# A state-space mixer on one core: block transfers within SBUF, a Toeplitz product for the taps, states as the stationary side

## The chip, the cores and the metric

The kernel runs on one core of one Trainium2 chip. The metric is the device time of one execution in microseconds (us). TensorE (PE, weight loads PEld), VectorE (DVE), ScalarE (ACT), GpSimd (POOL) and SyncE (SP) have their own instruction queues; each queue runs in order and waits on semaphores.

## The reference, cut to what matters

The network has two blocks over 256 tokens of width 1024. Block 1 is attention, pooling and a mixture of 16384 experts. Block 2 is a chain: FFN 0, the S5 mixer, FFN 1, FFN 2, attention (MoBA), FFN 3. The change is in the S5 mixer, with its preparation in block 1:

```
u = h @ w_in                                  # 256 x 1024: 64 groups g of 16 channels n
state[t] = lambda * state[t-1] + B u[t]       # complex, 64 states per group, lambda = exp(a dt)
y[t] = Re(C state[t]) + d * u[t]
g = gelu(y);  g = g * sigmoid(g @ w_glu);  out = g @ w_out
```

Both kernels cut the 256 steps into 32 chunks c of 8 steps s. Within a chunk, y depends on u through 8 taps K[k] = Re(C lambda^k B), a 16x16 matrix per group and k. Between chunks only the state at a chunk's start counts: "contribution" makes each chunk's input to the state, "the recurrence" carries the state over the 32 chunks with lambda^8, and "states out" turns the states into their share of y.

## The kernel before, in words

All weights are streamed from HBM in units of 128x1024 float32 by SP (`Stream`, L61) into four buffers, and split in a high part `wh` (ACT, L74) and a low part `wl` (DVE, L75), so that a product is three matmuls (L317 to L319, `mode_a`). The stream runs ahead as far as the buffers allow.

`s5_prep` (L943) is a generator that runs beside the expert phase of block 1. It makes lambda and its powers `lam`, `cw` (C lambda^k), `me` (B for the contribution), the taps `kr` (L1093 to L1099) and the powers of lambda^8, `pr` and `pi`, on POOL. Its tiles live in the large tile `act_lo`, so a profile's row names `act_lo` for all of them.

`s5_mixer` (L1115) runs after FFN 0:
- `u_tile(f)`, eight times: 24 matmuls for 128 channels (8 groups), a DVE product with the norm (L1155) into `uT`, a transfer to a DRAM tile `u_dram` (L1157), and after four of them eight transfers back (L1162) as `us`, with the 8 steps by 16 channels of a group on the partitions. All on SP's queue.
- `tap_weights(f)`: block-diagonal 128x128 tap matrices `s5kb`, by ACT (L1141) or POOL (L1143). `taps(f)`: 8 matmuls of falling width (L1174), copied by ACT to `yc` (L1176).
- `contribution(hf)`: 64 matmuls per half of the groups (L1187), `us` moving; two ACT copies into `ee[hf]` (L1189).
- `chunks(hf)`: the recurrence of a half on DVE (L1198 to L1220), in two blocks of 16 chunks side by side: 16 steps of four small operations, then four operations on 480 columns that carry the first block's end into the second.
- `spread(hf)`: states into a zeroed tile `s5sbd` (ACT L1236, DVE L1234). `states_out(qt)`: 16 matmuls with `cw` stationary (L1245), an ACT copy (L1250), and eight transfers to `y_dram` (L1253, SP and POOL); `states_in` reads them back with channels on the partitions (L1257).
- Sum with `yc` (DVE L1310), gelu (ACT L1311), split (L249, L250), then the eight GLU tiles `s5gps`, their sigmoid (L1319), the product (L1321), and `w_out`.

From `u_tile(6)` to the last `states_in`, PE and DVE keep the order in which the code is written (`manual_schedule`); `run(a, b)` puts a operations of the first half's recurrence and b of the second's there, in turn. Elsewhere, and on the other engines, a scheduler places instructions by priority.

Of the kernel before, what the change touches and what calls it, by code (L numbers as in the profile page):

```python
# [11 lines left out]
F32 = mybir.dt.float32  # L12
# [9 lines left out]
P = 128  # L22
# [105 lines left out]
class Net:  # L128
# [4 lines left out]
    def __init__(self, ctx, tc, i, out, tap=None):  # L133
# [18 lines left out]
        self.v_order = [*range(self.NLO, P), *range(self.NLO)]  # L152
        self.ada_late = list(range(5, 5 + 8 * 5, 5))
# [158 lines left out]
    def mode_a(self, ps, w, xh, xl):  # L312

        wh, wl = w
        for k in range(KT):
# [627 lines left out]
    def s5_prep(self, lo, hi):  # L943
# [140 lines left out]
        yield kr_end  # L1084

# [16 lines left out]

        pr, pi = keep(15, Q), keep(15, 2, Q)
# [9 lines left out]
        self.s5 = (lam, cw, me, kr, grp, pr, pi)  # L1113

    def s5_mixer(self):  # L1115
        nc, tc, i = self.nc, self.tc, self.i
        Q = 32
        lam, cw, me, kr, grp, pr, pi = self.s5
        with ExitStack() as st:
            wp = st.enter_context(tc.tile_pool(name="s5w", bufs=1))  # L1120
            dp = st.enter_context(tc.tile_pool(name="s5d", bufs=1, space=bass.MemoryType.DRAM))
            u_dram = dp.tile([64, 16, 8, Q], F32, name="u_dram")
            y_dram = dp.tile([64, 16, 8, Q], F32, name="y_dram")
            xh, xl = self.gained(self.cols[:, self.MIX_G : self.MIX_G + KT])
            rx = self.rstd()
            row = None
            l8 = wp.tile([P, 2, 2, Q], F32, name="s5l8")
# [4 lines left out]
            kbs = {}  # L1132

            uT = wp.tile([P, KT, 8, Q], F32, tag="sA", name="s5uT")
            us = wp.tile([P, 64, Q], F32, tag="sB", name="s5us")
            def tap_weights(f):
                kb = wp.tile([P, 8, 8, 16], F32, tag="s5kb", name="s5kb", bufs=5)
                k = kr[:, f].rearrange("p (k n) -> p k n", n=16)
                if f % 2:
                    for g in range(8):  # L1140
                        nc.scalar.activation(kb[:, :, g], k, AF.Copy, scale=grp[:, g : g + 1])  # L1141
                else:
                    nc.gpsimd.tensor_mul(kb, k.unsqueeze(2).to_broadcast([P, 8, 8, 16]),  # L1143
                                         grp[:, 0:8].unsqueeze(1).unsqueeze(3).to_broadcast([P, 8, 8, 16]))
                kbs[f] = kb

            for f in (0, 2):
                tap_weights(f)
            def u_tile(f):
# [3 lines left out]
                if row is None:  # L1153
                    row = self.rstd_row(wp, rx)
                nc.vector.tensor_mul(uT[:, f], ps.rearrange("p (c s) -> p s c", s=8),  # L1155
                                     row.rearrange("p (c s) -> p s c", s=8))
                nc.sync.dma_start(u_dram[8 * f : 8 * f + 8].rearrange("g n s c -> (g n) (s c)"),  # L1157
                                  uT[:, f].rearrange("p s c -> p (s c)"))
                if f % 4 == 3:
                    gs = slice(8 * f - 24, 8 * f + 8)  # L1160
                    for s in range(8):
                        nc.sync.dma_start(us[16 * s : 16 * s + 16, gs], u_dram[gs, :, s].rearrange("g n c -> n g c"))  # L1162

            yc = wp.tile([P, KT, S], F32, name="s5yc")
# [3 lines left out]

            def taps(f):

                kb = kbs.pop(f)
                ps = self.pm.tile([P, S], F32, tag="m", name="s5yps")
                for k in range(8):
                    nc.tensor.matmul(ps[:, k * Q :], kb[:, k].rearrange("p a b -> p (a b)"),  # L1174
                                     uT[:, f, 0 : 8 - k].rearrange("p s c -> p (s c)"), start=(k == 0), stop=(k == 7))
                nc.scalar.activation(yc[:, f], ps, AF.Copy)  # L1176

            def contribution(hf):

                for b in range(2):  # L1180
                    ps = self.pa.tile([P, 2, 8, Q], F32, tag=f"acc{2 * hf + b}", name="s5eps")
                    for q8 in range(8):
                        q = 16 * hf + 8 * b + q8
                        for half in range(2):
                            hs = slice(64 * half, 64 * half + 64)
                            for r in range(2):
                                nc.tensor.matmul(ps[hs, r, q8], me[q // 8][:, q % 8, r, hs], us[:, 2 * q + half], start=True, stop=True,  # L1187
                                                 tile_position=(0, 64 * half))
                    nc.scalar.activation(ee[hf][:, :, :, 8 * b : 8 * b + 8].rearrange("p c r q -> p r q c"), ps, AF.Copy)  # L1189

            def chunks(hf):
# [3 lines left out]
                s4 = ss[hf].rearrange("p (b c) r q -> p b c r q", b=2)  # L1195
                e4 = ee[hf].rearrange("p (b c) r q -> p b c r q", b=2)
                bl = lambda a: a.unsqueeze(1).to_broadcast([P, 2, 2, 16])
                yield v.memset(s4[:, :, 0], 0.0)  # L1198
                for c in range(16):
                    n = 2 if c < 15 else 1  # L1200
                    t = wp.tile([P, 2, 2, 2, 16], F32, tag=f"s5t{hf}", name="s5t")
                    t0, t1 = t[:, 0, :n], t[:, 1, :n]
                    if c < 15:
                        yield v.tensor_mul(t0, bl(l8[:, 0, :, qs]), s4[:, :, c])
                        yield v.tensor_mul(t1, bl(l8[:, 1, :, qs]), s4[:, :, c, ::-1])
                        yield v.tensor_add(t0, t0, e4[:, :, c])
                        yield v.tensor_add(s4[:, :, c + 1], t0, t1)
                    else:
                        t0, t1, end = t0[:, 0], t1[:, 0], s4[:, 1, 0]
# [61 lines left out]
            for f in range(6):  # L1271
                u_tile(f)
                if f in (1, 3):
                    tap_weights(f)
# [326 lines left out]
```

## Time and profile before

| | |
|---|---|
| time, median of 3 runs | 2143.38 us (2139.41 to 2146.39) |
| the profiled execution | 2139.12 us |
| its span in the profile | 2137.3 us |
| mean granted TensorE clock | 0.984 |
| S5 mixer, first instruction to the GLU's third tile | about 1279 to 1384 us of the span |

Times in the rows further down are from the span's start. A timeline row gives start, duration, engine, line, operation, output<-inputs, shape, count, and in brackets how long the engine had been idle and what ended that. Rows that follow each other closely are merged: the duration is then that of the whole stretch.

### The profile page before, as it was taken

How to read it: one execution, taken by the hardware profiler on the slowest of the kernel's cores; microseconds unless marked ns; L12 is line 12 of the kernel's file. 1: busy time of each engine (PE TensorE's matmuls, PEld its weight loads, DVE VectorE, ACT ScalarE, POOL GpSimd, SP SyncE). 2: the span in 40 equal slices, each digit the busy share in tenths (PEclk: the TensorE clock that was granted, in tenths of full speed). 3: DMA queues.
4: the chain of work that ended last, by engine and by line, in shares of the span. 5: the costliest groups of instructions: out<-in, count | busy, mean ns of one | idle time of the engine just before them, and what ended most of it. 6: DMA issues, size and time to landing. Idle time of an engine off the chain costs nothing. (4 is left out here: it accounts for less than half of the span.)

```text
span 2137.3 us, 35377 instructions
## 1 busy us (share of the span) xinstructions
PE 2021.1 (95%) x13270; PEld 1816.1 (85%) x13270; DVE 1520.3 (71%) x2808; ACT 1024.1 (48%) x1609; POOL 540.2 (25%) x548
## 2 busy tenths in 40 slices
PE   6889899999999899999999998899999999999999
PEld 4667899999999677788889988789998999778998
DVE  7987489887989666998765557465556555776555
ACT  4663545443444444555554444454444444565443
POOL 2333003037999332000131121101111111210111
PEclk9999999999999999999999999899999999999999
DMA  8763355554444877555555535355555555444552
GB/s 333 251 228 109 121 186 177 178 170 154 151 158 149 271 254 233 178 188 186 178 177 187 181 126 129 99 166 179 181 190 162 180 187 187 148 138 148 187 180 97
DMA packets 129564, 378.69 MB, mean 177 GB/s; under 512 B 26897, under 2 KB 41281, under 8 KB 129266
## 3 DMA queue, kind: packets, MB, share of 16 engines
q1 hardware_dynamic: 128160, 372.71, 53.0%
q0 software_dynamic: 1232, 3.73, 0.6%
q8 instruction: 104, 1.70, 0.3%
q14 instruction: 66, 0.54, 0.1%
q10 hardware_dynamic: 2, 0.00, 0.0%
HBM read 366.95 MB, written 9.44 MB: 176 GB/s over the span
## 5 line engine op out<-in xcount | busy, mean ns | idle before, releaser
L75 DVE TENSOR_TENSOR wl<-raw,wh 128x1024 fp32r<-128x1024 f32 (+1 forms) x595 | 751.4, 1264 | 312.3 <-ACT wh L74 309.3
L74 ACT ACTIVATE wh<-raw 128x1024 fp32r<-128x1024 f32 (+1 forms) x628 | 661.3, 1055 | 469.6 <-PE gups L318 165.7
L317 PE MATMUL gups<-xh,wh 128*128 128x256 f32 x1408 | 398.5, 284 | 6.4 <-ACT xh L305 3.1
L318 PE MATMUL gups<-xl,wh 128*128 128x256 f32 x1408 | 399.6, 284 | 2.3 <-DVE xl L306 2.3
L319 PE MATMUL gups<-xh,wl 128*128 128x256 f32 x1408 | 399.3, 284 | 0.7 <-DVE wl L75 0.5
L893 POOL TENSOR_TENSOR sgl<-sgl,rrow 128x256 f32<-128x256 f32 x88 | 126.3, 1435 | 735.2 <-ACT sgl L892 735.2
L317 PE MATMUL ups<-xh,wh 128*128 128x256 f32 x1024 | 293.6, 287 | 0.3 <-ACT act_lo L752 0.2
L319 PE MATMUL ups<-xh,wl 128*128 128x256 f32 x1024 | 290.0, 283 | 0.0
L318 PE MATMUL ups<-xl,wh 128*128 128x256 f32 x1024 | 289.7, 283 | 0.0
L317 PEld LDWEIGHTS gups<-xh,wh 128*128 128x128 f32 x1408 | 268.1, 191 | 12.0 <-ACT xh L305 4.8
L318 PEld LDWEIGHTS gups<-xl,wh 128*128 128x128 f32 x1408 | 268.1, 190 | 6.7 <-DVE xl L306 3.1
L319 PEld LDWEIGHTS gups<-xh,wl 128*128 128x128 f32 x1408 | 268.3, 191 | 1.1 <-DVE wl L75 1.1
L326 PE MATMUL acc<-wh,gl 128*128 128x512 f32 x512 | 201.6, 396 | 7.5 <-DVE gl L250 7.5
L324 PE MATMUL acc<-wh,gh 128*128 128x512 f32 x512 | 202.0, 395 | 2.5 <-ACT gh L249 2.0
L676 POOL TENSOR_SCALAR ob<-iota,idxT 128x128 f32<-128x128 f32 x256 | 194.6, 778 | 36.4 <-PE ups L319 32.2
L317 PEld LDWEIGHTS ups<-xh,wh 128*128 128x128 f32 x1024 | 194.1, 190 | 0.8 <-ACT act_lo L752 0.7
L318 PEld LDWEIGHTS ups<-xl,wh 128*128 128x128 f32 x1024 | 193.9, 189 | 0.1
L319 PEld LDWEIGHTS ups<-xh,wl 128*128 128x128 f32 x1024 | 193.9, 189 | 0.1
L325 PE MATMUL acc<-wl,gh 128*128 128x512 f32 x380 | 149.6, 394 | 0.7 <-DVE wl L75 0.7
L324 PE MATMUL acc<-wh,hh 128*128 128x512 f32 x352 | 139.3, 396 | 3.7 <-ACT hh L249 3.7
L326 PE MATMUL acc<-wh,hl 128*128 128x512 f32 x352 | 138.2, 394 | 0.4 <-DVE hl L250 0.3
L325 PE MATMUL acc<-wl,hh 128*128 128x512 f32 x352 | 138.5, 393 | 0.0
(395 smaller groups left out, 3390.1 us busy)
## 6 DMA issues: line engine op xcount, KB each, us to landing
raw<-peer_u SPq DMA_DIRECT2D x128, 512.0 KB, 3.5
raw<-peer_v SPq DMA_DIRECT2D x128, 512.0 KB, 3.6
raw<-ffn_gate SPq DMA_DIRECT2D x88, 512.0 KB, 4.3
raw<-ffn_up SPq DMA_DIRECT2D x88, 512.0 KB, 4.3
raw<-ffn_down SPq DMA_DIRECT2D x88, 512.0 KB, 3.5
raw<-w_ada SPq DMA_DIRECT2D x48, 512.0 KB, 5.2
raw<-w_in SPq DMA_DIRECT2D x24, 512.0 KB, 4.5
raw<-moba_w_qkv SPq DMA_DIRECT2D x24, 512.0 KB, 3.5
```

Source lines behind the costliest of these rows:

```text
L74: nc.scalar.activation(h[:, :n], raw[:, :n], AF.Copy)
L75: nc.vector.tensor_sub(lo[:, :n], raw[:, :n], h[:, :n].bitcast(F32))
L317: self.nc.tensor.matmul(ps, wh[:, s], xh[:, k], start=(k == 0), stop=False)
L318: self.nc.tensor.matmul(ps, wh[:, s], xl[:, k], start=False, stop=False)
L319: self.nc.tensor.matmul(ps, wl[:, s], xh[:, k], start=False, stop=(k == KT - 1))
L324: mm(acc, lh, wh, start=start, stop=False)
L325: mm(acc, lh, wl, start=False, stop=False)
L326: mm(acc, ll, wh, start=False, stop=stop)
L676: nc.gpsimd.tensor_scalar(b, iota, idx[:, 1, n : n + 1], None, ALU.is_equal)
L893: nc.gpsimd.tensor_mul(sg, sg, row)
```

## The change

In `s5_prep`, a DRAM tile `toep_dram` of 8 x 128 x 8 x 128 is filled: seven blocks with zeros, then for each step s the taps, shifted right by 16 s columns. So row (s, channel) of group g holds what one step's input gives to all 8 later steps: a 128x128 Toeplitz matrix per group and f. `load_taps(hf)` loads half of it (2 MB) as `s5tt` by eight POOL transfers; there is one buffer for both halves.

`w_in`'s columns are reordered on the host, so that u leaves the matmul with (channel, group) on the partitions, and `gather` moves it by transfers within SBUF, from `uT` to `us`, in three batches (f 0 to 3, 4 to 6, 7). The last batch is issued half by ACT. `u_dram`, `y_dram`, `tap_weights`, `yc` and `spread` are gone. `taps(hf)` is 32 matmuls with `us` stationary (32 columns, the chunks) and the Toeplitz matrix moving (128 columns). `states_out(hf)` is 64 matmuls with the states stationary (64 rows, 32 columns) and `cw` moving, added in the same PSUM tiles. ACT applies gelu from PSUM, DVE turns 32x32 blocks (STREAM_TRANSPOSE) to bring channels back to the partitions, and the split follows, half by half. The recurrence runs in four blocks of 8 chunks, and three block ends are carried on.

```
+        gp.memset(tw, 0.0)
+        for s in range(1, 8):
+            nc.gpsimd.dma_start(self.toep[s].rearrange("p f k -> p (f k)"), tw.rearrange("p a b c -> p (a b c)"))
...
+        for s in range(8):
+            nc.gpsimd.dma_start(self.toep[s, :, :, 16 * s :], kr[:, :, : P - 16 * s])
...
+            def load_taps(hf):
+                toeplitz[hf] = wp.tile([P, 8, 4, P], F32, tag="s5tt", name="s5tt")
+                for s in range(8):
+                    nc.gpsimd.dma_start(toeplitz[hf][16 * s : 16 * s + 16],
+                                        self.toep[s, :, 4 * hf : 4 * hf + 4].rearrange("(g n) f k -> n g f k", n=16))
...
+                    nc.gpsimd.tensor_copy(pw[:, hf, 0, :, r], pr[:, :8, qs])
+                    nc.gpsimd.tensor_copy(pw[:, hf, 1, :, r], pi[:, :8, r, qs])
...
-                nc.sync.dma_start(u_dram[8 * f : 8 * f + 8].rearrange("g n s c -> (g n) (s c)"),
-                                  uT[:, f].rearrange("p s c -> p (s c)"))
...
+            def gather(f0, f1):
+                for s in range(8):
+                    q = nc.scalar if f1 == KT and s % 2 else nc.sync
+                    q.dma_start(us[16 * s : 16 * s + 16, :, f0:f1].rearrange("p g f c -> p g (f c)"),
+                                uT[:, s, f0:f1].rearrange("p f c -> p (f c)"))
...
+                for c in range(8):
+                    n = 4 if c < 7 else 3
...
+                    yield v.tensor_mul(t0, bl(l8[:, 0, :, qs]), s4[:, :n, c])
+                    yield v.tensor_mul(t1, bl(l8[:, 1, :, qs]), s4[:, :n, c, ::-1])
+                    yield v.tensor_add(t0, t0, e4[:, :n, c])
+                    yield v.tensor_add(s4[:, :, c + 1] if c < 7 else s4[:, 1:, 0], t0, t1)
...
+                for b in (1, 2, 3):
+                    yield v.tensor_copy(sw[:, b - 1], s4[:, b, 0, ::-1])
+                    if b < 3:
+                        yield v.tensor_mul(t[:, 0], pw[:, hf, 0, 7], s4[:, b, 0])
+                        yield v.tensor_mul(t[:, 1], pw[:, hf, 1, 7], sw[:, b - 1])
+                        yield v.tensor_add(t[:, 0], t[:, 0], t[:, 1])
+                        yield v.tensor_add(s4[:, b + 1, 0], s4[:, b + 1, 0], t[:, 0])
...
+                yield v.tensor_mul(x[:, 0], powers(pw[:, hf, 0]), flat[:, 1:, 0].unsqueeze(2).to_broadcast(sh))
+                yield v.tensor_mul(x[:, 1], powers(pw[:, hf, 1]),
+                                   sw.rearrange("p b r q -> p b (r q)").unsqueeze(2).to_broadcast(sh))
+                yield v.tensor_add(x[:, 0], x[:, 0], x[:, 1])
+                yield v.tensor_add(flat[:, 1:, 1:], flat[:, 1:, 1:], x[:, 0])
...
+            def taps(hf):
...
+                for half in range(2):
+                    ps = yps[hf, half] = self.pa.tile([P, 4, P], F32, tag=f"acc{2 * hf + half}", name="s5yps")
+                    for f in range(4):
+                        for j in range(4):
+                            nc.tensor.matmul(ps[32 * j : 32 * j + 32, f], us[:, 2 * j + half, 4 * hf + f],
+                                             toeplitz[hf][:, 2 * j + half, f], start=(f == 0), stop=False,
+                                             tile_position=(0, 32 * j))
+            def states_out(hf):
...
+                            for j in range(4):
+                                q = 4 * (4 * hf + f) + j
+                                nc.tensor.matmul(yps[hf, half][32 * j : 32 * j + 32, f], ss[hf][hs, :, r, q % 16],
+                                                 cw[q // 8][hs, r, q % 8, 1:9].rearrange("p a b -> p (a b)"),
+                                                 start=False, stop=(f == 3 and r == 1), tile_position=(64 * half, 32 * j))
+                yg = wp.tile([P, Q, 2, 16], F32, tag=f"sE{hf}", name="s5yg")
+                for half in range(2):
+                    nc.scalar.activation(yg[:, :, half], yps[hf, half].rearrange("p f (s n) -> p (f s) n", n=16),
+                                         AF.Gelu_apprx_tanh)
+                for f in (0, 2):
+                    fs = slice(4 * hf + f, 4 * hf + f + 2)
+                    nc.vector.transpose(yt[:, fs].rearrange("p f t -> p (f t)"),
+                                        yg[:, 8 * f : 8 * f + 16].rearrange("p a b c -> p (a b c)"))
+                    self.split(gh[:, fs], gl[:, fs], yt[:, fs])
...
+            for f in range(4):
                 u_tile(f)
+            gather(0, 4)
+            u_tile(4)
+            u_tile(5)
+            contribution(0)
             u_tile(6)
+            gather(4, 7)
+            run(6)
             u_tile(7)
+            gather(7, 8)
             taps(0)
+            load_taps(1)
+            run(24)
+            contribution(1)
             taps(1)
+            run(99, 17)
+            states_out(0)
             run(0, 99)
             states_out(1)
+            first = [(self.pm.tile([P, S], F32, tag="m", name="s5gps"), self.stream.next()) for _ in range(2)]
+            for ks in (range(4), range(4, KT)):
+                for ps, w in first:
+                    self.mode_a(ps, w, gh, gl, ks)
```

On SP's queue, around the projection of u, the rows before were these (`raw` is the weight stream):

```order
L61 DMA raw<-s_w_glu 128x1024
L1162 DMA s5us<-u_dram 16x32x32 x8
L1157 DMA u_dram<-s5uT 128x256 x3
L61 DMA raw<-s_w_glu 128x1024
L1157 DMA u_dram<-s5uT 128x256
L61 DMA raw<-s_w_glu 128x1024 x2
L1162 DMA s5us<-u_dram 16x32x32 x8
L61 DMA raw<-s_w_glu 128x1024
L1253 DMA y_dram<-s5ys 16x16x32 x10
```

and with the change, in the same place:

```order
L61 DMA raw<-s_w_in 128x1024 x8
L61 DMA raw<-s_w_glu 128x1024
L1171 DMA s5us<-s5uT 16x8x128 x8
L61 DMA raw<-s_w_glu 128x1024 x3
L1171 DMA s5us<-s5uT 16x8x96 x8
L1171 DMA s5us<-s5uT 16x8x32 x4
L61 DMA raw<-s_w_glu 128x1024
```

The eight writes and sixteen reads by way of DRAM have become twenty SBUF transfers (four more stand on ACT's queue), of 128 pieces each instead of 512.

On DVE, at the end of the recurrence's second half (`s5s` the states, `s5x` the carry, `s5yt` y by channels), the rows before were these:

```order
L1217 TENSOR_TENSOR s5x<-act_lo,s5s 128x480
L1218 TENSOR_TENSOR s5x<-act_lo,s5s 128x480
L1219 TENSOR_TENSOR s5s<-s5s,s5x 128x480
L1220 TENSOR_TENSOR s5s<-s5s,s5x 128x480
L1234 COPY s5sbd<-s5s 64x32x32
L1310 TENSOR_TENSOR s5yt<-s5yt,s5yc 128x256 x2
L250 TENSOR_TENSOR xl<-s5yt,xh 128x256 x2
```

With the change, these stand where the first half ends:

```order
L1206 TENSOR_TENSOR s5s<-s5t 128x4x32
L1224 TENSOR_TENSOR s5s<-s5s,s5x 128x3x224
L1255 STREAM_TRANSPOSE s5yt<-s5yg 128x512
L252 TENSOR_TENSOR xl<-s5yt,xh 128x512
L1255 STREAM_TRANSPOSE s5yt<-s5yg 128x512
L252 TENSOR_TENSOR xl<-s5yt,xh 128x512
L1203 TENSOR_TENSOR s5t<-s5l_13770,s5s 128x128
L1204 TENSOR_TENSOR s5t<-s5l_13770,s5s 128x128
```

The first half's turns and low parts (L1255, L252) now stand ahead of the last 31 operations of the second half's recurrence, which begin with L1203.

On POOL, between block 1 and FFN 0 (`x_sb` the residual, `sgl` FFN 0's gate), nothing stood before; with the change the taps' writes do:

```order
L480 TENSOR_TENSOR x_sb<-x_sb,upd 128x512 x2
L1109 DMA toep_dram<-act_lo 128x1024
L1109 DMA toep_dram<-act_lo 1024x1x112
L1109 DMA toep_dram<-act_lo 1024x1x96
L1109 DMA toep_dram<-act_lo 1024x1x80
L1109 DMA toep_dram<-act_lo 1024x1x64
L1109 DMA toep_dram<-act_lo 1024x1x48
L1109 DMA toep_dram<-act_lo 1024x1x32
L1109 DMA toep_dram<-act_lo 1024x1x16
L895 TENSOR_TENSOR sgl<-sgl,rrow 128x256 x22
L1139 DMA s5tt<-toep_dram 16x8x512 x8
```

Seven of the eight write 1024 pieces each, and FFN 0's first gate stands behind them.

## Rows read from the trace of the kernel before

**Rows 1.** Page, part 1: busy us, share of the span, instructions.

```profile
PE 2021.1 (95%) x13270; PEld 1816.1 (85%) x13270; DVE 1520.3 (71%) x2808; ACT 1024.1 (48%) x1609; POOL 540.2 (25%) x548
```

**Rows 2.** Engines by stretch: span, length, busy (instructions) per engine, clock, DMA share.

```profile
1340.60:1352.30 11.70, 9.07 (x48) 8.90 (x47) 10.81 (x48) 4.65 (x4) 0.00 (x0) 0.66 0.01 1
1352.30:1372.30 20.00, 16.57 (x129) 16.10 (x127) 0.99 (x4) 7.11 (x12) 6.77 (x12) 0.93 0.35 66
```

**Rows 3.** Timeline of DVE in the S5 mixer.

```profile
1282.19 1.45 DVE L1129 COPY s5l<-act_lo 128x32 f32<-128x32 f32 x2
1283.56 1.90 DVE L1130 TENSOR_SCALAR s5l<-act_lo 128x32 f32<-128x32 f32 x1
1285.38 0.17 DVE L1131 COPY s5l<-act_lo 128x32 f32<-128x32 f32 x1
...
1301.56 0.67 DVE L1155 TENSOR_TENSOR s5uT<-s5ups,rrow 128x256 f32<-128x256 f32 x1 [0.65 <-PE s5ups L319]
...
1307.25 0.67 DVE L1155 TENSOR_TENSOR s5uT<-s5ups,rrow 128x256 f32<-128x256 f32 x1 [0.64 <-PE s5ups L319]
...
1313.95 1.22 DVE L75 TENSOR_TENSOR wl<-raw,wh 128x1024 fp32r<-128x1024 f32 x1
...
1319.09 0.23 DVE L1204 TENSOR_TENSOR s5t<-s5l,s5s 128x64 f32<-128x64 f32 x1
...
1319.88 0.23 DVE L1204 TENSOR_TENSOR s5t<-s5l,s5s 128x64 f32<-128x64 f32 x1
...
1339.98 0.65 DVE L1220 TENSOR_TENSOR s5s<-s5s,s5x 128x480 f32<-128x480 f32 x1
...
1365.18 0.76 DVE L1310 TENSOR_TENSOR s5yt<-s5yt,s5yc 128x256 f32<-128x256 f32 x2 [12.71 <-DMA s5yt<-y_dram]
```

**Rows 4.** Timeline of PE: the preparation's last matmuls, and the S5 mixer.

```profile
1078.58 3.77 PE L1093 MATMUL tps<-act_lo,gate_hi 128*32 128x128 f32 x128
...
1313.52 3.93 PE L1187 MATMUL s5eps<-s5us,act_lo 128*64 128x32 f32 x128 [0.61 <-DMA u_dram<-s5uT]
...
1326.10 6.03 PE L1187 MATMUL s5eps<-s5us,act_lo 128*64 128x32 f32 x128 [3.94 <-DMA s5us<-u_dram]
...
1361.87 7.36 PE L1245 MATMUL s5sps<-s5sbd,act_lo 128*128 128x64 f32 x64 [0.41 <-ACT s5sbd L1236]
...
1384.12 0.38 PE L317 MATMUL s5gps<-xh,wh 128*128 128x256 f32 x1 [1.90 <-ACT s5sg L1319]
```

**Rows 5.** Timeline of SP's queue.

```profile
1299.40 0.32 SPq L1157 DMA_DIRECT2D u_dram<-s5uT  x1
...
1305.04 4.36 SPq L1162 DMA_DIRECT2D s5us<-u_dram  x8
```

**Rows 6.** DMA issues: output<-input, queue, count, KB each, median us to landing.

```profile
s5us<-u_dram SPq DMA_DIRECT2D x16, 64.0 KB, 4.4
...
y_dram<-s5ys SPq DMA_DIRECT2D x20, 32.0 KB, 2.0
```

**Rows 7.** Timeline of ACT in the S5 mixer.

```profile
1317.48 1.05 ACT L1189 ACTIVATE s5e<-s5eps 128x512 f32<-128x512 f32 x1 [0.74 <-PE s5eps L1187]
...
1351.99 0.60 ACT L1250 ACTIVATE s5ys<-s5sps 128x512 f32<-128x512 f32 x1 [6.89 <-PE s5sps L1245]
...
1381.31 1.06 ACT L74 ACTIVATE wh<-raw 128x1024 fp32r<-128x1024 f32 x1 [0.98 <-PE s5gps L318]
1382.38 1.28 ACT L1319 ACT_TABLE_LOAD   x1
```

**Rows 8.** Timeline of POOL: FFN 0's first gate, and the S5 mixer.

```profile
1099.35 0.74 POOL L893 TENSOR_TENSOR sgl<-sgl,rrow 128x256 f32<-128x256 f32 x1 [17.84 <-ACT sgl L892]
...
1279.71 5.72 POOL L1143 TENSOR_TENSOR s5kb<-act_lo 128x1024 f32<-128x1024 f32 x3 [4.15 <-PE acc L326]
...
1352.89 1.76 POOL L1253 DMA_DIRECT2D y_dram<-s5ys  x3 [28.64 <-ACT s5ys L1250]
```

**Rows 9.** Timeline of DVE: the last operations on the taps `kr`.

```profile
1084.02 0.67 DVE L125 SCALAR_TENSOR_TENSOR act_lo<-act_lo,cols_sb 128x16 f32<-128x16 f32 x4
```

More of the change, by code (lines that the diff above doesn't have):

```diff
@@ L310, in gained, with mode_a @@
         return xh, xl
-    def mode_a(self, ps, w, xh, xl):
+    def mode_a(self, ps, w, xh, xl, ks=range(KT)):
         wh, wl = w
-        for k in range(KT):
+        for k in ks:
             s = slice(k * P, k * P + P)
@@ L1112, in s5_prep @@
         gp.tensor_scalar(pi[:, :, 0], pi[:, :, 1], -1.0, None, ALU.mult)
-        self.s5 = (lam, cw, me, kr, grp, pr, pi)
+        self.s5 = (lam, cw, me, pr, pi)
     def s5_mixer(self):
@@ L1131, in s5_mixer @@
             nc.vector.tensor_copy(l8[:, 1, 1], lam[:, 1, 8])
[L1132 to L1148, printed above, removed]
+            pw = wp.tile([P, 2, 2, 8, 2, 16], F32, name="s5pw")
+            for hf in range(2):
+                qs = slice(16 * hf, 16 * hf + 16)
+                for r in range(2):
+                    nc.gpsimd.tensor_copy(pw[:, hf, 0, :, r], pr[:, :8, qs])
+                    nc.gpsimd.tensor_copy(pw[:, hf, 1, :, r], pi[:, :8, r, qs])
+            uT = wp.tile([P, 8, KT, Q], F32, tag="sA", name="s5uT")
+            us = wp.tile([P, 8, KT, Q], F32, tag="sB", name="s5us")
             def u_tile(f):
@@ L1167, in s5_mixer @@
             ss = [both[:, hf] for hf in range(2)]
[L1169 to L1176, printed above, removed]
             def contribution(hf):
@@ L1308, in s5_mixer @@
-            gh, gl = self.xt_tiles()
-            for f in range(KT):
-                nc.vector.tensor_add(yt[:, f], yt[:, f], yc[:, f])
-                nc.scalar.activation(yt[:, f], yt[:, f], AF.Gelu_apprx_tanh)
-                self.split(gh[:, f], gl[:, f], yt[:, f])
+            states_out(1)
             oh = wp.tile([P, KT, S], F32R, tag="sA", name="s5oh")
             ol = wp.tile([P, KT, S], F32R, tag="sS", name="s5ol")
-            for f in range(KT):
-                ps = self.pm.tile([P, S], F32, tag="m", name="s5gps")
-                self.mode_a(ps, self.stream.next(), gh, gl)
+            first = [(self.pm.tile([P, S], F32, tag="m", name="s5gps"), self.stream.next()) for _ in range(2)]
@@ L1318, in s5_mixer @@
+            for ks in (range(4), range(4, KT)):
+                for ps, w in first:
+                    self.mode_a(ps, w, gh, gl, ks)
+            in_order.close()
+            for f in range(KT):
+                if f < 2:
+                    ps = first[f][0]
+                else:
+                    ps = self.pm.tile([P, S], F32, tag="m", name="s5gps")
+                    self.mode_a(ps, self.stream.next(), gh, gl)
                 sg = wp.tile([P, S], F32, tag="s5sg", name="s5sg", bufs=2)
```

118 lines of the change are left out of this document (24 added, 94 removed).

## The prediction

> **What bounds the kernel now.** I read the page's busy shares first, then the stretches of the S5 mixer, then the timeline of each engine there. PE is busy for 95% of the span [rows 1], so elsewhere the kernel is paced by matmuls and the weight stream, which the change leaves alone. The mixer's middle is the exception. From 1340.60 to 1352.30 DVE is busy for 10.81 of 11.70 us: PE works at a granted clock of 0.66 and waits for the second half of the recurrence. From 1352.30 to 1372.30 DVE does 0.99 us of work in 20 [rows 2], and its next operation waits 12.71 us for y to come back from DRAM [rows 3]. Ahead of that, PE's second contribution waited 3.94 us for u to come back [rows 4]. The stage is a chain: u by way of DRAM, contribution, recurrence, states out, y by way of DRAM, gelu, GLU. So I follow that chain through the changed order to one mark: the first matmul of the GLU's third tile, which starts at 1384.12 [rows 4]. From there on both kernels do the same. Times below are on the axis of the trace of before.
>
> **The start of the mixer.** POOL's tap weights go (5.72 us [rows 8]); beside them two DVE copies took 1.45 us and the next 1.90, where the third, alone, took 0.17 [rows 3]. POOL now issues the taps' load there and copies eight small pieces. I take 2.8 us off (1.45 + 1.90 less three times 0.17); if the new POOL work holds DVE as the old did, it is nothing. ACT's 32 tap weights go too; they lay beside other work.
>
> **u.** `u_tile(3)`'s product ends at 1301.56 + 0.67 [rows 3], now 1299.4. Eight transfers follow on SP. An issue of 128 pieces took 0.32 us, one of 512 pieces 4.36 / 8 = 0.55 [rows 5]; the new ones have 128, I take 0.36, 2.9 in all. Landing: 2.0 us as the 32 KB writes, at most 4.4 as the reads of before [rows 6]. So u is there at 1304.3. PE ends `u_tile(5)` at 1307.25 [rows 3] less 2.8 = 1304.4, so contribution 0 need not wait; it takes 3.93 us [rows 4] and ends at 1308.4. Two more u tiles at 2.85 us each (1307.25 - 1301.56 is two tiles [rows 3]) end at 1311.2 and 1314.1.
>
> On DVE: the product of tile 6 until 1311.9, six recurrence operations, a low part of 1.22, the product of tile 7 until 1315.0. A step of four operations on 64 columns took 1319.88 - 1319.09 = 0.79 us; from 0.23 us at 64 columns to 0.65 at 480 [rows 3] a column costs 1.0 ns, so a step on 128 takes 1.05, an operation on 512 about 0.68 and one on 672 about 0.85. 24 operations (6.3) and eight more (1.4) end at 1322.7. The last batch of u is issued from 1315.0 (four each on SP and ACT, 1.4 us) and lands at 1318.4. PE did `taps(0)` meanwhile: 32 matmuls in the shape of the preparation's, 64 of which (two instructions each) took 3.77 us, 59 ns a matmul [rows 4], so 1.9 us until 1316.0. Contribution 1 took 3.93 us warm and 6.03 after an idle PE [rows 4]; I take 5, then ACT's copy of 1.05 [rows 7] and 0.1 of handoff: 1324.6. DVE then has 28 operations, both halves in turn: 14 on 128 columns at 0.2, ten small ones at 0.13 (an estimate, two thirds of that), four large ones at 0.8: 7.3 us. The first half's recurrence ends at 1331.9, against 1340.63 before (1339.98 + 0.65 [rows 3]).
>
> `taps(1)` has to be done by then. Its load is issued on POOL once `taps(0)` has freed the buffer, 8 x 0.59 (1.76 / 3 [rows 8]) = 4.7 us, 1320.7, with 4 us to land, 1325, then 1.9 to 2.9 on PE: hidden with 4 us to spare.
>
> **The tail.** Here the order matters: the turns of half 0 stand on DVE ahead of the rest of half 1.
> - States out 0: 64 matmuls. The trace has none with 64 rows and 32 columns; the nearest, 32 columns in four column groups, gives 59 ns, 3.8 us warm; the last of before, full width, 7.36 / 64 = 115 ns per instruction, two a matmul [rows 4], which is 14.7 us. I take the first, the nearer shape, and half of the cold surcharge of the contributions: 5.0. 1336.9.
> - Table load 1.28, then two gelus on 512 columns, 0.60 to 1.05 [rows 7], I take 0.8, and handoffs 0.2: 1340.0.
> - Turn, split, turn, split: DVE 4 x 0.68, ACT 2 x 0.60 [rows 7], handoffs 0.4: 4.3 us. A 32x32 turn is not in the trace; a copy's rate halved or doubled puts 0.34 to 1.36 on each of the two. 1344.3.
> - The 31 operations left of half 1, alone: four steps 4.2, eleven small ones at 0.2, four large ones 3.3: 9.7. 1354.0.
> - States out 1, PE cold: 5.8. Gelus 1.8, turns 4.3: 1365.9.
> - The low part of the GLU's second weight stands behind the turns: 1.2 [rows 3]. Then 24 matmuls until the first tile is whole, 0.12 us warm (2.85 / 24), 0.16 with a part of them cold: 3.8. Then ACT's 1.06 and 1.28 [rows 7] and 0.5 for the sigmoid: 1373.7 for the third tile.
>
> That is 10.4 us earlier. From the recurrence's end to the mark it was 43.5 us and is 41.8, so the 20 us of the round trip by DRAM are nearly all given back to the second half's recurrence, which now stands behind half 0's turns, and to a PE that cools beside it. What is won is won ahead of that.
>
> **Outside the mixer** I cost nothing. The zeros (3.7 MB) are written in the expert phase, where POOL has idle time. The taps are ready at 1084.7 (1084.02 + 0.67 [rows 9]) and FFN 0's first gate needs POOL at 1099.35 [rows 8]: eight issues at 0.59 fill 4.7 of 14.6 us. If an issue grows with its pieces, fourfold, it is 7 x 2.35 + 0.59 = 17 us, and FFN 0 starts 2.5 us later, since its first down product waits for that gate. The 7 x 1024 small writes share the DMA engines with the weights, eight units ahead there.
>
> **Sum.** 2139.1 (the profiled execution) - 10.4 = 2128.7. That execution lies 4.3 below the median of the runs shown, so against the median 2143.4 - 10.4 = 2133.0, my forecast. Low end: states out warm both times (-3.2), turns and gelus at their lower prices (-2.2), contribution 1 warm (-1.1), small operations overlapped better (-2), three more for handoffs and a warm GLU: 2121. High end with the mechanism intact: nothing at the start (+2.8), u landing as the reads of before and issues of 0.55 (+7.1 over both batches), turns and gelus high (+4), FFN 0 (+2.5): 2149.
>
> The Trainium skill, "DMA: Bandwidth & Descriptors", section Specifications, wants pieces of at least 512 bytes for line rate. In this trace the reads with pieces of 128 bytes landed in 4.4 us and the writes to DRAM with such pieces in 2.0 [rows 6], so it does not decide alone. By that rule the batches of 384 and 128 bytes would take the longer time: 2.4 us on the forecast.
>
> **Rivals.**
> 1. *The taps come late, no change.* POOL issues its load beside a busy DVE. For: DVE operations stretched from 0.17 to 1.90 beside POOL [rows 3]; if each of the eight issues is held as long (+1.73), they end at 1316.0 + 18.6 = 1334.6, the load lands at 1338.6, `taps(1)` ends at 1341.5, and states out 0 behind it on PE starts 9.6 later: 2142.6. Against: the rows show DVE held, not POOL's issue, and the three issues at 1352.89 had an idle DVE. The Trainium skill, "SBUF — State Buffer", section on a bandwidth-pool intuition that's wrong, has it that descriptors from GpSimd wait for a VectorE operation that holds the shared port, with 620 ns grown to 3100; by that figure the forecast would be some 14 us later, an estimate. No row here shows a POOL issue beside the recurrence.
> 2. *Slower: the state matmuls do not overlap.* Row groups of 64 with column groups of 32 have no row here. If they run one after the other at 115 ns per instruction, both states out take 14.7 instead of 5.0 and 5.8: +18.6, 2151.6. It decides from 140 ns a matmul on, where the 10.4 us are gone (128 matmuls, 81 ns more each). For: full-width products of 64 columns cost that much. Against: the preparation's products in column groups took 59 ns.
> 3. *The change doesn't speed u up.* SBUF transfers with twenty issues in front of the contributions land as late as before: the start's 2.8 and the tail's 1.7 us remain, 2138.9. For: contribution 0 has 0.1 us of slack. Against: a whole write and its wait fall away.
>
> **Chances.** Forecast as described 0.60, taps late 0.15, serial states 0.15, late u 0.10. Within 0.3% (6.4 us) is about what a measurement here cannot tell from no change. Of the forecast's 0.60, 0.47 lies below 2137.0 and 0.13 above. Late taps: 0.12 same, 0.03 slower; serial states: slower; late u: 0.05 faster, 0.04 same, 0.01 slower. Together faster 0.52, same 0.29, slower 0.19. The range, 2121 to 2152, takes in all the rivals' times and the ends of the unknown prices.
>
> **What would show it.** Right: contribution 0 directly behind `u_tile(5)`; L1246's 64 matmuls in 4 to 6 us; a DVE without work between the end of half 0 (near 1332) and its first STREAM_TRANSPOSE, for some 8 us; 31 operations of half 1 after the turns with an idle PE; the third GLU tile near 1374. Wrong: PE waiting for `s5us` for more than 2 us, `taps(1)` waiting for `s5tt`, a first gate of FFN 0 later than 1102, or states out above 9 us. The forecast fails most easily on PE's price for the state matmuls and on how long a turn takes.

## The result, and the profile after

The changed kernel is slower: 2153.93 us median (2152.99 to 2155.22, 4 runs) against 2142.11 (4 runs), ratio 1.0055 with a 95% interval of 1.004 to 1.007, where the forecast was 2133.0. The profiled execution took 2155.22 us, its span is 2153.4.

Page of after, part 1, for [rows 1]: every engine but POOL is busy for less time, yet the span is longer.

```profile
PE 2001.5 (93%) x13398; PEld 1795.6 (83%) x13398; DVE 1515.3 (70%) x2757; ACT 1003.5 (47%) x1554; POOL 544.4 (25%) x570
```

Timeline of PE in after, for [rows 4]: the preparation's last matmuls, the two contributions (the second in two pieces), the two states out, the GLU's third tile.

```profile
1085.76 3.77 PE L1098 MATMUL tps<-act_lo,gate_hi 128*32 128x128 f32 x128
...
1320.33 6.47 PE L1187 MATMUL s5eps<-s5us,act_lo 128*64 128x32 f32 x128 [4.77 <-DMA s5us<-s5uT]
...
1350.04 5.35 PE L1187 MATMUL s5eps<-s5us,act_lo 128*64 128x32 f32 x96 [15.39 <-DMA s5us<-s5uT]
1357.88 1.93 PE L1187 MATMUL s5eps<-s5us,act_lo 128*64 128x32 f32 x32 [2.49 <-DMA s5us<-s5uT]
...
1368.16 3.70 PE L1246 MATMUL s5yps<-act_lo,s5s 64*32 64x128 f32 x128 [4.78 <-DVE s5s L1224]
...
1387.86 3.40 PE L1246 MATMUL s5yps<-act_lo,s5s 64*32 64x128 f32 x128 [15.99 <-DVE s5s L1224]
...
1404.84 0.39 PE L319 MATMUL s5gps<-xh,wh 128*128 128x256 f32 x1 [1.30 <-ACT s5sg L1309]
```

The preparation's matmuls stand 7.2 us later than in before, ahead of anything in the mixer. So I measure the mixer from the residual add at its start (`x_sb`, the first of the four that close FFN 0) to the mark, the first matmul of the GLU's third tile. The adds, of before and of after (timeline of DVE):

```profile
1277.52 0.69 DVE L867 SCALAR_TENSOR_TENSOR x_sb<-acc,x_sb 128x512 f32<-128x512 f32 x1 [0.59 <-PE acc L326]
```

```profile
1285.02 0.69 DVE L869 SCALAR_TENSOR_TENSOR x_sb<-acc,x_sb 128x512 f32<-128x512 f32 x1 [0.59 <-PE acc L328]
```

The stretch was 1384.12 - 1277.52 = 106.60 us and is 1404.84 - 1285.02 = 119.82, 13.2 longer; the forecast had 96.2. Behind the mark after needs 748.6 us to its span's end, before 753.2. In the sixteen profiles of this case that remainder lies between 748.6 and 753.3 and the add between 1277.5 and 1290.6. Single executions alone differ by several us there (e8, e14 and e9, nearly one program, have the add at 1281.4, 1283.7 and 1287.4), so the stretch is what to compare. Before's add is the earliest of all sixteen; e5 comes back to that.

What is late in it is u. SP's queue in after, for [rows 5], and the landing of the transfers, for [rows 6]:

```profile
1309.49 8.86 SPq L1171 DMA_DIRECT2D s5us<-s5uT  x8
...
1330.62 18.28 SPq L1171 DMA_DIRECT2D s5us<-s5uT  x12
```

```profile
s5tt<-toep_dram POOLq DMA_DIRECT2D x16, 256.0 KB, 12.2
...
s5us<-s5uT SPq DMA_DIRECT2D x8, 64.0 KB, 6.3
...
s5us<-s5uT SPq DMA_DIRECT2D x8, 48.0 KB, 3.2
s5us<-s5uT ACTq DMA_DIRECT2D x4, 16.0 KB, 6.2
s5us<-s5uT SPq DMA_DIRECT2D x4, 16.0 KB, 12.8
```

From one issue to the next it takes 1.1 us in the first row (8.86 / 8) and 1.5 in the second (18.28 / 12), where I had 0.36, and a transfer of 16 KB lands after 12.8. The issuing instruction itself takes 0.55 to 0.9 us, but for one of 1.23 and one of 1.61. The rest is waiting: each issue names a semaphore that its transfer raises on landing, SP and ACT use the same few of them in turn, and the next issue on a semaphore waits for that landing. Who SP's queue waited for (engine, line, awaited, us in total, times, longest), and the two longest such waits, whose issues followed 20 ns behind the landing of transfers of u that ACT had issued (1341.44 and 1347.69):

```profile
SPq L1171 <- DMA s5us<-s5uT: 9.6, 3, 5.7
```

```profile
1341.46 0.55 SPq L1171 DMA_DIRECT2D s5us<-s5uT  x1
...
1347.71 0.55 SPq L1171 DMA_DIRECT2D s5us<-s5uT  x1
```

What the DMA engines do meanwhile, by stretch (columns as in [rows 2]; the last three are clock, DMA share, GB/s), and POOL's issues, with FFN 0's first gate for [rows 8]:

```profile
1335.00:1340.00 5.00, 0.00 (x0) 0.00 (x0) 4.66 (x20) 0.00 (x0) 4.16 (x8) 0.96 0.91 128
1340.00:1345.00 5.00, 0.00 (x0) 0.00 (x0) 1.21 (x8) 0.00 (x0) 0.00 (x0) 0.50 1.09 120
1345.00:1350.00 5.00, 0.00 (x0) 0.00 (x0) 0.00 (x0) 0.00 (x0) 0.00 (x0) 0.50 1.11 122
```

```profile
1092.39 6.80 POOL L1109 DMA_DIRECT2D toep_dram<-act_lo  x8 [3.70 <-ACT wh L74]
1106.85 0.74 POOL L895 TENSOR_TENSOR sgl<-sgl,rrow 128x256 f32<-128x256 f32 x1 [7.66 <-ACT sgl L894]
...
1287.67 4.24 POOL L1139 DMA_DIRECT2D s5tt<-toep_dram  x8 [4.61 <-DVE x_sb L869]
...
1334.98 4.18 POOL L1139 DMA_DIRECT2D s5tt<-toep_dram  x8 [41.14 <-PE s5yps L1234]
```

From 1340 to 1350 no engine works but for 1.2 us of DVE; the DMA engines are full, at 121 GB/s: the second load of the taps, issued from 4.4 us behind the first of u's last transfers on.

### The profile page after: what moved, and what is told of

The parts are those of the page before. It is cut to its first block, busy times and chain, and to the rows that moved or that the text cites. A ratio compares the mean times of both kernels' runs of the same rounds, so it can differ in the third digit from the quotient of the medians.

```text
span 2153.4 us, 35517 instructions
## 1 busy us (share of the span) xinstructions
PE 2001.5 (93%) x13398; PEld 1795.6 (83%) x13398; DVE 1515.3 (70%) x2757; ACT 1003.5 (47%) x1554; POOL 544.4 (25%) x570
## 3 DMA queue, kind: packets, MB, share of 16 engines
q1 hardware_dynamic: 114912, 369.89, 51.9%
```

## Experiments

Stretch is from the residual add to the third tile; the column before it is how far behind the add contribution 1 starts; both are in us, from one profile each. Ratios are to the runs of before on the same chip, with 95% intervals.

| kernel | median us | ratio | contribution 1 | stretch |
|---|---|---|---|---|
| before | 2142.11 | | 48.6 | 106.6 |
| after | 2153.93 | 1.0055 (1.004 to 1.007) | 65.0 | 119.8 |
| e1 | 2144.6 | 1.002 (1.0001 to 1.0039) | 55.2 | 107.4 |
| e2 | 2149.16 | 1.0035 (1.0016 to 1.0054) | 52.5 | 116.1 |
| e3 | 2172.16 | 1.0141 (1.0108 to 1.0175) | 78.3 | 130.8 |
| e4 | 2152.4 | 1.0056 (1.0038 to 1.0074) | 68.6 | 121.2 |
| e5 | 2145.96 | 1.0007 (0.9991 to 1.0023) | 49.3 | 107.9 |
| e6 | 2146.16 | 1.0014 (0.9998 to 1.003) | 56.6 | 107.4 |
| e7 | 2141.57 | 0.9995 (0.9977 to 1.0014) | 52.9 | 104.3 |
| e8 | 2124.61 | 0.992 (0.9892 to 0.9948) | 51.9 | 91.0 |
| e9 | 2131.0 | 0.9945 (0.993 to 0.9961) | 52.9 | 90.2 |
| e10 | 2138.91 | 0.9986 (0.9967 to 1.0005) | 67.6 | 107.3 |
| e11 | 2137.22 | 0.9977 (0.9959 to 0.9995) | 46.9 | 99.7 |
| e12 | 2140.15 | 0.9993 (0.9975 to 1.0011) | 61.0 | 101.6 |
| e13 | 2125.75 | 0.9925 (0.9901 to 0.9949) | 47.4 | 89.2 |
| e14 | 2128.54 | 0.9939 (0.9916 to 0.9963) | 53.4 | 90.5 |

**e1, the taps' loads by group.** The same bytes, pieces and count, but each transfer in 128 partitions.

```
-  for s in range(8):
-      nc.gpsimd.dma_start(toeplitz[hf][16 * s : 16 * s + 16], self.toep[s, :, 4 * hf : 4 * hf + 4].rearrange("(g n) f k -> n g f k", n=16))
+  for g in range(8):
+      nc.gpsimd.dma_start(toeplitz[hf][:, g], self.toep[:, 16 * g : 16 * g + 16, 4 * hf : 4 * hf + 4])
```

> The loads of the taps (load_taps, 2 MB each) are cut by group instead of by phase: eight transfers as before, pieces of 2 KB as before, but each ends in all 128 partitions where it ended in 16. Theory A: the loads of the taps are what makes u late. In the trace of after the DMA engines are full at some 120 GB/s from 1290 to 1308 and from 1335 to 1358, which is when the two loads run, and the weights of the mixer and the transfers of u stand in the same engines. Then both loads end in 6 to 9 us, contribution 1 starts 10 to 16 us earlier, from the mixer's first residual add to the first matmul of the GLU's third tile it takes 103 to 109 us instead of 119.8, and the time is 2138 to 2144. Theory B: u's transfers from SBUF to SBUF are slow by themselves (1.1 us to issue one). Then this changes 0 to 4 us: 2150 to 2154. Theory C, on the 7.5 us that were gone before the mixer: if they are the zeros written to the taps' tensor, they are gone here too, and the mixer's residual add lies 7 us later than in before; if they are the spread of one execution, it lies anywhere from -3 to +7.

The stretch fell by 12.4 us, to what A said; the time is 0.6 us above A's range, and the loads were less improved than it had: 2 MB at 212 GB/s is 10 us. The edit changes the order of the rows read in DRAM as well as the partitions written; no run separates the two. Stretch and second contribution of e1:

```profile
1336.00:1340.00 4.00, 0.00 (x0) 0.00 (x0) 0.48 (x4) 0.00 (x0) 0.00 (x0) 0.50 1.07 212
```

```profile
1340.17 6.32 PE L1186 MATMUL s5eps<-s5us,act_lo 128*64 128x32 f32 x128 [10.26 <-DMA s5us<-s5uT]
```

**e2, the second load held until u is there** (a copy of one column of `us` into the taps' tile on POOL, ahead of the load, makes it wait).

> The load of the second half's taps is held back on POOL until the last batch of u has landed; nothing else is changed. Theory A (the loads of the taps are in u's way): contribution 1 starts within 8 us of the last u product instead of 17 us after it, but the load then runs alone for 17 to 20 us behind it and taps(1) becomes what is late: states out 0 comes between 3 us earlier and 5 us later than in after, time 2150 to 2159. Theory B (u's transfers are slow by themselves): contribution 1 starts as late as in after, 15 us or more behind the last u product, and the load comes on top: 2165 to 2175.

A again, with a time 0.8 us below its range: contribution 1 waits 4.42 us for u instead of 15.39, and the load, now alone, is late in its turn. That contribution, and stretches of e2 with nothing else in the DMA engines:

```profile
1335.94 5.49 PE L1189 MATMUL s5eps<-s5us,act_lo 128*64 128x32 f32 x128 [4.42 <-DMA s5us<-s5uT]
```

```profile
1348.00:1352.00 4.00, 0.00 (x0) 0.00 (x0) 1.68 (x3) 0.00 (x0) 0.00 (x0) 0.50 1.03 115
1352.00:1356.00 4.00, 0.00 (x0) 0.00 (x0) 0.00 (x0) 0.00 (x0) 0.00 (x0) 0.50 1.04 116
```

So the engines are full at 115 GB/s by the load's own shape: 2 MB take 18 us.

**e3, u by way of DRAM; e4, u's transfers into every eighth partition** (`us[s : P : 8]`). In e3 too the contraction meets u in another order, so the values differ.

> u goes by way of DRAM as in the kernel before (eight writes, then the gather's transfers read it back in the same batches and on the same queues); taps, states and turns stay as in after. Theory A: no gain, the reads stand behind the loads of the taps as the transfers within SBUF did, and a write and its wait come on top: 2153 to 2160. Theory B: the reads land in 4 to 5 us as in before: contribution 1 starts 8 to 12 us earlier than in after, 2142 to 2147.

> u's transfers end in every eighth partition (16 of them, over the whole array) instead of 16 neighbours; their number, bytes and pieces are the same. The contraction then meets u in another order than its other operand, so the values differ. Theory A: the transfers of u still stand behind the loads of the taps, 0 to 3 us less: 2150 to 2154. Theory B, in the form that 16 neighbouring partitions make u's transfers slow: the first batch lands 4 us and the second 8 to 12 us earlier, 2141 to 2146.

e3 went A's way by more than A said: 11 us more of stretch than after; a write's landing comes on top of the reads' (medians 7.0 us for the writes, 13.2 for the reads of the second batch). e4 gained nothing (1.4 us more of stretch): where u's transfers end is not the cause. B falls with both.

**e5, the kernel before with the taps' writes** (the clearing and the shifted taps, fifteen transfers that nothing reads).

> The kernel before, with only the taps' writes of the change added to the preparation: the clearing of the tensor in DRAM (7 x 512 KB) and the eight transfers of the shifted taps; nothing reads them. Theory C: these writes are what the changed kernel lost ahead of the mixer. It is then 4 to 7 us slower than before, 2145 to 2148, the first gate of FFN 0 comes 4 us or more after 1099.35, and where the zeros are written PE is idle or at a lower granted clock. Rival: the writes lie beside work and cost 0 to 2 us, 2140 to 2143; the place of the mixer's first residual add is then the spread of one execution.

+0.07%, from -0.09% to +0.23%, which is -2 to +5 us: C's 4 to 7 is nearly out, the rival's 0 to 2 is not told from it. In its one profile C's signs are there: FFN 0's first gate comes at 1106.09, 6.7 us behind 1099.35, and the add stands late too. But that execution took 2146.45 us, while before's own beside it ran from 2137 to 2148, and of before there is one profile only, so the place of the add decides less than I wrote.

```profile
1106.09 0.74 POOL L895 TENSOR_TENSOR sgl<-sgl,rrow 128x256 f32<-128x256 f32 x1 [10.51 <-ACT sgl L894]
```

```profile
1284.27 0.69 DVE L869 SCALAR_TENSOR_TENSOR x_sb<-acc,x_sb 128x512 f32<-128x512 f32 x1 [0.59 <-PE acc L328]
```

Beside the zeros (900 to 905) and beside the shifted taps (1095 to 1100) the granted clock was 0.66 for 5 us each, 1.00 in before: 1.7 us each, if it is their doing. A second estimate, from the table: after and the other thirteen changed kernels take on average 1.2 us more, against before, than their stretches give (from -3.7 to +5.9). So the writes cost little outside the mixer; that they cost nothing isn't shown.

**e6, `taps(0)` directly behind contribution 0, so that the second load starts earlier; e7, e6 with each batch on SP and ACT** (`q = nc.scalar if s % 2 else nc.sync`).

> The taps' loads by group as in e1, and taps(0) moved on PE from behind u_tile(7) to directly behind contribution 0, so that the buffer is free and the second load issued some 6 us earlier, ahead of the last batches of u instead of beside them. If the load is still in u's way in e1 (there contribution 1 waited 10.26 us for u, with the load issued 4.3 us behind the gather's first), contribution 1 starts 3 to 6 us earlier, at 1334 to 1337 where the mixer's residual add is at 1285, and the time is 2138 to 2142. If what is left in e1 is the price of issuing the twelve transfers (12 us on SP), contribution 1 stays within 2 us of e1: 2143 to 2146.

> As e6, and each batch of u's transfers is issued on two queues, four on SP and four on ACT, where only the last batch was. If issuing is what is left (0.65 us each in e1, 0.78 in e2, where the forecast had 0.36), the first batch is there 2 to 3 us and the last 3 to 5 us earlier than in e6: 2133 to 2138. Rival: ACT stops at its four issues until the product of u is there and brings the next weights late, so that PE waits for a weight about 2 us: no better than e6, 2138 to 2143.

e6 gained nothing: the load, 10 us long, now overlaps the last batches from its other end. By its number that spoke for the price of issuing; e13 shows that reading to be wrong. In e6 SP stopped after four issues of the second batch until the first of them had landed (1332.74; the next issue is at 1332.76). e7 took 3 us off the stretch (its time met the rival's), through the first batch: contribution 0 waits 1.21 us for u, not 2.28, and takes 3.93 us, not 5.48.

**e8, DVE's order.** Half 0's recurrence to its end, half 1's to its end, then the turns.

```
-  run(24)
+  run(99)
   contribution(1)
   taps(1)
-  run(99, 17)
+  run(0, 99)
   ...
   states_out(0)
-  run(0, 99)
   states_out(1)
```

> As e7, and DVE runs the first half's recurrence to its end before it begins the second half's, and the second half's to its end before the turns of the first half. In e1 PE waited 16.0 us between the two states out, 4.1 of them for half 0's turns on DVE, and half 0's recurrence was held by the second contribution, with which it runs in turn. If the order on DVE is what the tail hangs on: states out 1 starts within 16 us of the end of contribution 1 (27.9 us in e1), 8 to 13 us are gained on e7: 2122 to 2130. Rival: operations that run in turn hide each other's latency, and one half alone is slower by 0.06 us an operation (some 5 us over 80 operations): 2129 to 2134.

13.3 us off e7's stretch, 2124.61, and faster than before beyond its interval. PE's second states out starts 14.5 us behind the end of contribution 1 (the first, at a granted clock of 1.00, and the second, at 0.50):

```profile
1342.20 2.24 PE L1245 MATMUL s5yps<-act_lo,s5s 64*32 64x128 f32 x128
...
1354.50 3.71 PE L1245 MATMUL s5yps<-act_lo,s5s 64*32 64x128 f32 x128 [10.05 <-DVE s5s L1223]
```

**e10, that order alone, in the changed kernel.**

> The changed kernel with DVE's order of e8 alone: half 0's recurrence to its end, half 1's to its end, then the turns; the taps' loads stay by phase in 16 partitions, and u's transfers as they were. If the order is worth what e8 against e7 shows (17 us), and u's lateness is a sum of its own: 2135 to 2141. Rival: with u as late as it is (contribution 1 ends at 1359.7) half 0's recurrence is done long before, and the order gives back part of the time that u costs: 2130 to 2135. If the order only pays where u is early: 2145 to 2152.

12.5 us off the stretch of after, with u as late as ever: the sums are nearly independent, and the third reading (it pays only where u is early) falls.

**e11, no loads of the taps.**

> The changed kernel without the two loads of the taps: the tile is cleared once and both halves use it, so the convolution's part of the output is left out; everything else is as it was. Theory A: what is left is what the forecast had, but for the price of issuing u's transfers (0.65 to 0.78 us each where the forecast had 0.36: some 3 us on each batch): contribution 0 waits less than 4 us for u, contribution 1 less than 9, from the mixer's residual add to the third GLU tile 97 to 103 us (the forecast had 96.2, the changed kernel 119.8), time 2132 to 2140. If u's transfers are slow by themselves, contribution 1 still waits 12 us or more, and the mixer takes over 108 us: 2143 or more.

As A had it. The two contributions of e11, SP's first eight issues and the landing of its 16 KB transfers:

```profile
1315.70 3.93 PE L1188 MATMUL s5eps<-s5us,act_lo 128*64 128x32 f32 x128 [2.22 <-DMA s5us<-s5uT]
...
1331.80 6.85 PE L1188 MATMUL s5eps<-s5us,act_lo 128*64 128x32 f32 x128 [4.40 <-DMA s5us<-s5uT]
```

```profile
1308.56 5.16 SPq L1172 DMA_DIRECT2D s5us<-s5uT  x8
```

```profile
s5us<-s5uT SPq DMA_DIRECT2D x4, 16.0 KB, 1.9
```

The loads cost 119.8 - 99.7 = 20.1 us of the stretch, all of the loss and more.

**e12, e8 with u by way of DRAM.**

> As e8, but u goes by way of DRAM (a write for each tile, then the same number of reads in the same batches on the same queues, with pieces of 512 bytes and less). What do the transfers within SBUF give? The write has to land before the reads begin, 2 to 4 us on each batch. Contribution 0 starts 2 to 5 us later than in e8, contribution 1 3 to 8 us later: 2127 to 2133. If both ways are equal, because the engines of the transfers and not the memory set the time: 2123 to 2127.

Ten us more of stretch than in e8: the way within SBUF is worth more than I expected. The write of `u_tile(6)` stands beside the load and takes 8.84 us to land; the reads behind it land in 2.3 to 2.8.

**e9, e13, e14.** e9 was to hold the second load in e8 behind u, but its copied column was in the way of one of eight transfers; the others were issued before, and e9 is e8 in effect. e13 holds all eight (`toeplitz[hf][:, :, 0, :1]` from `us[:, :, 7, :1]`); e14 repeats e8.

> As e8, with the second load of the taps held on POOL until the last batch of u has landed (in e8 the load runs from 1318 to 1331, and contribution 1 waits 9.3 us for u beside it). If that load is the whole of what makes u late there: contribution 1 starts within 6 us of the last u product (8.9 us in e8). DVE is busy with half 0's recurrence until 16 us behind the first recurrence operation in either case, so little of it reaches the end: 2121 to 2126. If the issue of the transfers is the rest, contribution 1 starts 8 us or more behind the product, and the time is 2123 to 2130, since the load now ends later.

> e9 held only the first of the load's eight transfers; the other seven were issued beside u's last batches (1325.14 to 1329.26), and contribution 1 waited 9.5 us as in e8. Here all eight wait for u. If the load by group is what keeps u in e8: contribution 1 starts 3 to 6 us behind the last u product (9 us in e8 and e9), as it did in e2 and in e11 (4.4 us of waiting); the load then ends some 10 us behind u, taps(1) with it, still ahead of the end of half 1's recurrence: 2122 to 2128. If contribution 1 still starts 8 us or more behind the product, issuing is the cause.

> The kernel e8 once more, beside e13, for the difference to before: four fast runs gave 2124.6, and e9, which is nearly the same program, gave 2131.0 on another chip. If e8 is faster than before as its stretch of the mixer says (91.0 us from the residual add to the third GLU tile, 106.6 in before): 14 to 17 us faster than the runs of before beside it, 2125 to 2130.

e13's contribution 1:

```profile
1332.26 3.93 PE L1188 MATMUL s5eps<-s5us,act_lo 128*64 128x32 f32 x128 [2.90 <-DMA s5us<-s5uT]
```

So what is left in e1 and e6 to e9 is the load beside u, not the issuing. It acts twice: u's transfers land behind it, and the next batch isn't issued before they have landed (SP waited 7.2 us for that in e7; in e13 the issues of the last two batches wait for no landing). Issues took 2.61 / 4 = 0.65 us on SP and 2.92 / 4 = 0.73 on ACT (the first batch of e13).

Little of it reaches the end. Contribution 1 starts 4.5 to 6 us earlier in e13 than in e8, e9 and e14, and the stretch is 1.0 to 1.8 us shorter: in e13 DVE is at half 0's recurrence until 1342.7, 6.5 us behind the end of contribution 1, and the held load is late for `taps(1)`, which waits for it four times:

```profile
1340.08 0.38 PE L1235 MATMUL s5yps<-s5tt,s5us 128*32 128x128 f32 x2 [3.89 <-DMA s5tt<-toep_dram]
```

By their ratios e8, e9, e13 and e14 are 12 to 17 us faster than before; e13 and e14 can't be told apart. These are the versions that beat both kernels.

## Why the prediction was wrong

The step that failed is the one on **u**: "Landing: 2.0 us as the 32 KB writes, at most 4.4 as the reads of before", with issues at 0.36. Contribution 1 was to begin 40.9 us behind the add and began 65.0 behind it. It is not only a size that slipped: the mechanism was missing. I asked of the taps' loads whether *they* would be late ("hidden with 4 us to spare", and rival 1), never what they do to the transfers and weights beside them. The 2.0 us of [rows 6] came from a stretch with a DMA share of 0.35 [rows 2]. Two loads of 2 MB, each some 18 us of full engines, were free in my sum; e11 puts them at 20 us. The load's own term was wrong too: "4 us to land" had the second load done 9 us behind its first issue, and it took 22.1 (1334.98 to 1357.09); `taps(1)` still didn't wait for it, because u was later. Rival 3 named the symptom, u not sped up, but with the late times of before as its worst case, and 0.10 on it. Rival 1 is out: POOL's eight issues took 4.18 us with DVE busy for 4.66 of 5, and 4.24 at the start. Of the signs of being wrong, PE's wait for `s5us` (15.39 us) and the late gate (1106.85) came; the two prices on which I thought the forecast would fail most easily, state matmuls and turn, did not fail it.

By steps, on the stretch from the add:

- *Start of the mixer* (-2.8): DVE's three copies are as short as said, 0.26 for two and 0.17 (rows below, for [rows 3]), but the saving doesn't reach u. `u_tile(3)`'s product ends 24.4 us behind the add, 24.7 in before, and I had 21.9. On DVE two low parts of weights stand ahead of the first products, one in before; PE waited 2.90 us for the products instead of 0.84, and the granted clock was 0.64 for the next 4.7 us, 1.00 in before (rows below). e11 has this too (23.6), so 1.7 of these 2.5 us are not the loads'. PE's sixth u tile then ends 3.6 us later than forecast (30.5 us behind the add, 26.9; 28.6 in e11): weights stand beside the first load, and ACT waited 3.45 and 2.14 us for them.
- *Contribution 0*: forecast 26.9 us behind the add, was 35.3. Of the 8.4, 2.5 are that later product and the rest u's transfers: 10.7 us from the product's end to the last landing, where I had 4.9. In e11 30.8, with 7.0 us for the transfers (5.16 for eight issues, where I had 2.9). So the load is 4.5 of the 8.4.
- *Contribution 1*: +24.1, of which 18.1 go without the loads (46.9 in e11).
- *Recurrence from there*: 8.3 us (1359.81 to 1368.10), forecast 8.5.
- *States out*: 3.70 and 3.40 us for 64 matmuls, 58 and 53 ns each, at a granted clock of 0.50 and 0.56; forecast 5.0 and 5.8. Rival 2 is out. At a clock of 1.00 they take 35 ns (e8's first states out), less than the nearer shape's 59.
- *Turns and gelus*: table 1.28 and two gelus 1.09 together (forecast 1.6), a turn 0.71 (0.68), the four steps of turn and split 4.1 (4.3).
- *Rest of half 1*: 1378.37 to 1387.81, 9.4 (9.7).
- *Tail*, recurrence's end to the mark: 36.7, forecast 41.8. My remark that half 0's turns ahead of the rest of half 1 give back what the round trip by DRAM saved was right, and worth more than I made of it: e10 gets 12.5 us for the order alone.
- *Outside the mixer* (nothing): e5 allows -2 to +5 us. POOL issued the shifted taps at 0.85 us each, and FFN 0's gate did not wait for them (its wait of 7.66 us is for ACT). The 7.2 us that after's profile shows there are no more than before's executions differ by (2137 to 2148 beside e5).

Sum: 96.2 + 28.7 up to the recurrence's end - 5.1 in the tail = 119.8.

Timeline of PE at the start, of before and of after; the granted clock of after from there (columns as above):

```profile
1295.58 0.36 PE L317 MATMUL s5ups<-xh,wh 128*128 128x256 f32 x1 [0.84 <-DVE s5uT L1155]
```

```profile
1301.29 0.36 PE L319 MATMUL s5ups<-xh,wh 128*128 128x256 f32 x1 [2.90 <-DVE s5uT L1165]
```

```profile
1301.30:1306.00 4.70, 4.70 (x27) 4.70 (x28) 0.45 (x2) 0.20 (x1) 0.00 (x0) 0.64 1.00 142
```

Timeline of DVE in after: the start, the end of half 0's recurrence, the first turn.

```profile
1289.39 0.26 DVE L1145 COPY s5l<-act_lo 128x32 f32<-128x32 f32 x2
1290.34 0.17 DVE L1146 TENSOR_SCALAR s5l<-act_lo 128x32 f32<-128x32 f32 x1
1290.43 0.17 DVE L1147 COPY s5l<-act_lo 128x32 f32<-128x32 f32 x1
...
1367.25 0.85 DVE L1224 TENSOR_TENSOR s5s<-s5s,s5x 128x672 f32<-128x672 f32 x1
...
1374.35 0.71 DVE L1255 STREAM_TRANSPOSE s5yt<-s5yg 128x512 f32<-128x512 f32 x1 [6.24 <-ACT s5yg L1251]
```

Timeline of ACT in after, for [rows 7]:

```profile
1371.93 1.28 ACT L1251 ACT_TABLE_LOAD   x1 [11.01 <-PE s5yps L1246]
1373.23 1.09 ACT L1251 ACTIVATE s5yg<-s5yps 128x512 f32<-128x512 f32 x2
```

The load at 115 GB/s with full engines is what I could have read in advance. The Trainium skill, "SBUF — State Buffer", section Door 1: The DMA port swizzle, has it that a transfer reaches only the ports of the partitions it spans: 104 GB/s measured for 16 partitions, 328 for 128, with transfers of 1 MiB. The trace is near the first (115 and 116 in e2) and lower than the second (212 in e1), with 256 KB a transfer. The Trainium skill, "DMA: Bandwidth & Descriptors", section Issuing engines are not separate DMA queues, adds that transfers of all issuing engines interleave on the same 16. The trace agrees: SP's 16 KB transfers landed in 12.8 us beside POOL's load, in 1.9 without it.

## What to carry to other kernels

A load that is hidden for its own reader is not free: add up what runs in the DMA engines during its time, and ask which small transfer on the critical chain stands among it. Cut a large load so that each transfer spans all partitions (12.4 us of stretch here, e1). Holding it back, with a true dependence, until the small urgent transfer has landed frees that transfer, but only pays if the load isn't late then (3.7 us of stretch in e2, 1 to 2 in e13). Look at what the queue of an urgent transfer waits for: it can be the landing of an earlier one, whose semaphore the next is to use. Where two halves of a chain share an engine, finish the chain that the end hangs on before the epilogue of the other half (12.5 and 13.3 us of stretch in e10 and e8).

## What the runs showed of the hardware

- A load of 2 MB by transfers into 16 partitions each fills all 16 DMA engines at 115 GB/s; into 128 partitions, with the same pieces, 212.
- The issue of a transfer within SBUF, with 128 pieces, took 0.55 to 0.9 us on SP and ACT, beside the load (after) as without it (e11), with few longer ones (up to 1.6). What grew beside the load was the wait ahead of an issue for the landing of an earlier transfer on the same semaphore, and with it the wait of what stands behind on that engine (ACT's next weight stood 13.07 us behind eight such issues in e7, 5.83 in e13).
- Pieces of 384 and 128 bytes between SBUF and SBUF landed in 1.9 to 2.4 us when nothing stood beside them (e13).
- Matmuls with 64 rows and 32 columns in eight places of the array took 58 ns each at a granted clock of 0.50 and 35 at 1.00 (the two rows of e8).
- Executions of one kernel lie up to 17 us apart (before on the chip of e9 to e12: 2134.2 to 2150.85). The place of the add differs by 13 us between the profiles (1277.5 to 1290.6), the remainder behind the mark by 5. Stretches of one profile compare better than spans.
